# A transformer kernel of four blocks on one core: entry without the norm's factor, experts sent back in pairs, and GpSimd left with powers alone

## The chip, the cores and the metric

One of the eight cores of a Trainium2 chip runs the whole program. The metric is device time in microseconds (us) of one execution; 1 core means that there is no other core to wait for. TensorE multiplies, VectorE (DVE) and ScalarE (ACT) do elementwise work, GpSimd (POOL) too, and SyncE (SP) starts the transfers of weights.

## The reference

256 tokens of width 1024, batch 1, all in float32. Four blocks run one after another, each of which adds to x:

```python
h = rmsnorm(x, norm_mix[0]);  x += short_conv_mixer(h)     # layer 0
h = rmsnorm(x, norm_ffn[0]);  x += swiglu(h)               # 2816 wide
h = rmsnorm(x, norm_mix[1]);  x += mla_mixer(h)            # layer 1, 8 heads
h = rmsnorm(x, norm_ffn[1]);  x += moe_swiglu(h)           # 8 experts, 2 chosen, 2048 wide
h = rmsnorm_2(x, attn_norm_g); x += two_attentions(h)      # 8 query heads on 2 key heads; 4 differential heads
h = rmsnorm_2(x, mlp_norm_g);  x += square(relu(h @ w_up)) @ w_down    # 4096 wide

def rmsnorm(x, g):
    return x * rsqrt(mean(x * x) + EPS) * g
def short_conv_mixer(h):
    b, c, u = split(h @ w_in, 3)
    v = c * u
    conv = w[0] * v[t-2] + w[1] * v[t-1] + w[2] * v[t]
    return (b * conv) @ w_out
```

c, u and b are each linear in h, so a token's factor 1/rms can be left out of h: v then lacks the factor twice, 1/ms with ms = mean(x*x)+EPS, and the output lacks it once more. The expert block sends each token to the two best of eight experts, gathers an expert's tokens into up to 128 slots, and adds the gated results back.

## The kernel before

**Two halves of every number.** Float32 operands of the large products are split into a high part (w_hi, cast by ScalarE to fp32r, line 115) and the rest (w_lo, a subtraction on VectorE, line 116). A product is three: hi x hi, lo x hi, hi x lo (mm3, line 231). All weights pass through split() in the order that the generator weight_parts (line 159) writes out. load() (line 96) starts a transfer of 1 MB on SP's queue into one of RAW_BUFS = 7 raw buffers; during the expert stage three more (pool raws2, line 845) take turns with them, loads 8 to 10 of each ten (line 100). get() hands out the next split pair and keeps one more ahead; prepare(n) (line 216) makes sure that n are in the making. behind(...) and the list fence set an instruction behind others in the order that the framework's planner gives each engine; what is not so bound the planner orders by itself.

**Start.** x comes in four quarters of 128 tokens x 512 features, the first 128 tokens before the others (lines 65, 82). The gain row is spread over the partitions by a product with ones (line 560). first_norm (line 358) squares x on ScalarE, takes the power -1/2 on GpSimd (line 350), multiplies x by factor and gain on VectorE (line 374), transposes on TensorE (line 377) and splits into hT hi and lo (lines 379, 384). proj_T (line 236) makes 2 x 128 output features from two weight pairs, 24 products each. The conv loop (line 565) takes for each pair of feature blocks c (copied by ScalarE, line 568), u, then b, and forms the convolution on VectorE. Entry (line 397) is the transition to the next block: for each half of the tokens it adds the accumulated output to x (line 425), multiplies by the gain, transposes, splits, and takes squares and power; half(0) at once, half(1) in finish(), which the next block calls when its first products are issued.

**Experts** (line 1083). For g = 0 to 32, four chunks of 512 for each of 8 experts: gate and up of chunk g, then down of chunk g-1, which sums into two banks yb over an expert. When an expert's down is whole, gated_y (line 1049) splits yb into y; scatter (line 1057) sends it back to the tokens, 8 products of 512 columns and 4 additions into x, after gate and up of the next chunk. Every second expert, gather (line 1017) fetches the inputs of the next two by products with the 0/1 matrix pick, copied out by ScalarE (hi) and VectorE (lo). The last expert's scatter goes into the Entry of the second attention through enter (line 1126).

**Second attention** (line 1134). columns_in makes 256 columns of the input projection; the first call does one half of the tokens, then rest_of_entry, then the other. Generators keys_a, queries_a, heads_a and so on are advanced one step at a time by a table (line 1357), so that their steps alternate with the projections. rotate2 (line 1187) ends with an addition on GpSimd (line 1198); heads_a divides each head's exponentials by their sum on GpSimd (line 1301); the powers of all norms are GpSimd's too (lines 434, 1185, 1349). The differential heads divide on VectorE (line 1333).

Of the kernel before, what the change touches and what calls it, by code (L numbers as in the profile page):

```python
# [18 lines left out]
P = 128  # L19
# [22 lines left out]
def block_kernel(ctx: ExitStack, tc: tile.TileContext, i, out):  # L42
# [38 lines left out]
    for ns in blocks(2, 512):  # L81
        nc.sync.dma_start(x[:, 1, ns], i["x"][0, P:, ns])
# [43 lines left out]
    def columns_of(w):  # L126

        for c in range(0, w.shape[1], 256):
# [30 lines left out]
    def weight_parts():  # L159

        w = i["conv_w_in"][0]
        upper = [columns_of(w[:, g * D : (g + 1) * D]) for g in (1, 2, 0)]
        for _ in range(0, KD, 2):
            for u in upper:
                yield next(u)
                yield next(u)
# [69 lines left out]
    def proj_T(h, fresh=False):  # L236

        o = bank().rearrange("p (f t) -> p f t", f=2)
        for f in range(2):
            hi, lo = get()  # L240
            late, early = ((hi, h[1]), (lo, h[0])) if fresh and f == 0 else ((lo, h[0]), (hi, h[1]))
            for k in range(KD):
                mm(o[:, f], hi[:, k], h[0][:, k], k == 0, False)
            for k in range(KD):
                mm(o[:, f], early[0][:, k], early[1][:, k], False, False)
            for k in range(KD):
                mm(o[:, f], late[0][:, k], late[1][:, k], False, k == KD - 1)
        return o

# [108 lines left out]
    def first_norm(g):  # L358

        hi, lo = h_pair()  # L360
        xn = acts.tile([P, 2, D], F32, tag="xn", name="xn", bufs=1)
        factors = []
        for t in range(2):
            ss = small.tile([P, 2], F32, name="ss")
            for n, ns in enumerate(blocks(2, 512)):
                nc.scalar.activation(xn[:, t, ns], x[:, t, ns], AF.Square, accum_out=ss[:, n : n + 1])
            ms = small.tile([P, 1], F32, name="ms")
            nc.vector.tensor_scalar(ms, ss[:, 0:1], ss[:, 1:2], 1.0 / D, op0=OP.add, op1=OP.mult)
            nc.vector.tensor_scalar(ms, ms, EPS, None, op0=OP.add)
            factors.append(power(ms, 1))  # L370
        turned, copies = [], []
        for t, ts in enumerate(blocks(2)):
            for n, ns in enumerate(blocks(2, 512)):
                nc.vector.scalar_tensor_tensor(xn[:, t, ns], x[:, t, ns], factors[t], g[n], op0=OP.mult, op1=OP.mult)
                v = bank().rearrange("p (k t) -> p k t", k=4)
                for k in range(4):
                    nc.tensor.transpose(v[:, k], xn[:, t, (4 * n + k) * P : (4 * n + k + 1) * P], ident)
                hv, lv = (z[:, 4 * n : 4 * n + 4, ts] for z in (hi, lo))
                copies = copies[-1:] + [(nc.vector.tensor_copy if len(turned) == 3 else nc.scalar.copy)(hv, v)]
                turned.append((lv, v, hv))  # L380
        fence[:] = copies
        prepare(1)
        for lv, v, hv in turned:
            last = nc.vector.tensor_tensor(lv, v, hv.bitcast(F32), op=OP.subtract)
        fence[:] = [last]
        return hi, lo
# [10 lines left out]
    class Entry:  # L397
# [5 lines left out]
        def __init__(self):  # L403
# [3 lines left out]
            self.ss, self.ms, self.rs = (small.tile([P, 2], F32, name=n) for n in ("ss", "ms2", "rs2"))  # L407

# [10 lines left out]
        def enter(self, t, acc):  # L419
# [3 lines left out]
            for n, ns in enumerate(blocks(2, 512)):  # L423
                if acc is not None:
# [1033 lines left out]
```

## Time and profile before

| | |
|---|---|
| runs, us | 1303.44, 1300.73, 1299.24 (median 1300.73) |
| profiled execution | 1304.09 us, its span 1302.3 us, mean granted clock 0.992 |
| TensorE (PE) busy | 1267.9 us, 97% |
| VectorE busy | 994.9 us, 76% |
| ScalarE busy | 801.7 us, 62% |
| GpSimd busy | 76.3 us, 6%, 96 instructions |
| read from memory | 317 MB, 245 GB/s over the span |

A busy TensorE counts overlapping products once; where its share is whole, the pace of the products decides. "Idle before" a group is the time in which its engine did nothing just ahead of it, with the instruction that ended it. L377 is line 377 of the kernel.

### The profile page before, as it was taken

The numbers are of one execution on the slowest core, as the hardware profiler recorded it, in microseconds if no ns is written. First come the engines' busy times: TensorE is split into PE (matmuls) and PEld (weight loads), VectorE is DVE, ScalarE is ACT, GpSimd is POOL, SyncE is SP. The second block draws the span as 40 slices with busy tenths as digits, with TensorE's granted clock in tenths as the row PEclk, the third lists the DMA queues.
The fourth block names the chain that finished last, engine by engine and source line by source line (L and its number), as shares of the span: only waits on it lengthen the run. The fifth ranks groups of instructions, "written<-read, shape, count | busy, mean of one in ns | idle before, by whom it ended". The sixth has DMA issues, their size and how long they took to land.

```text
span 1302.3 us, 17506 instructions
## 1 busy us (share of the span) xinstructions
PE 1267.9 (97%) x6551; PEld 1065.9 (82%) x6551; DVE 994.9 (76%) x1283; ACT 801.7 (62%) x1089; POOL 76.3 (6%) x96
## 2 busy tenths in 40 slices
PE   8999999999998999999999999999998999999998
PEld 7998788888777888888888887878787887888887
DVE  6665655556867999999988989898898697765654
ACT  5444445445665877778867776777766566544442
POOL 0000100000502000000000000000000432000000
PEclk9999999999998999999999999999998999999999
DMA  9854655744434999989999999989987533456620
GB/s 318 280 168 175 217 192 129 245 142 149 163 127 174 372 379 353 374 306 360 356 335 320 326 359 337 349 324 361 349 307 243 177 106 114 144 188 196 192 97 33
DMA packets 156799, 320.26 MB, mean 246 GB/s; under 512 B 7788, under 2 KB 50823, under 8 KB 156712
## 3 DMA queue, kind: packets, MB, share of 16 engines
q1 hardware_dynamic: 151104, 313.54, 68.5%
q10 hardware_dynamic: 5608, 5.58, 1.8%
q8 instruction: 52, 0.85, 0.3%
q14 instruction: 35, 0.29, 0.1%
HBM read 317.00 MB, written 2.10 MB: 245 GB/s over the span
## 4 chain that ended last, share of the span: by engine, by line
PE 62%; DVE 2%; ACT 1%; POOL 1%; DMA 1%; issue 1%; POOLq 0%; ACTq 0%
PE bank L58 38%; PE yb L58 13%; PE acc L58 8%; PE bank L1076 1%; DVE w_lo L116 1%; PE po L58 1%; ACT w_hi L115 1%; DMA bias<-wide_d 1%; POOL yq L1198 0%; DMA raw<-in_moe_w_up_dram 0%; PE bank L1279 0%; POOL s L1301 0%; ACT s L1295 0%; POOL raq L1185 0%; PE bank L392 0%
## 5 line engine op out<-in xcount | busy, mean ns | idle before, releaser
L116 DVE TENSOR_TENSOR w_lo<-raw,w_hi 128x1024 fp32r<-128x1024 f32 (+2 forms) x600 | 709.6, 1218 | 189.6 <-ACT w_hi L115 177.4
L115 ACT CAST w_hi<-raw 128x1024 fp32r<-128x1024 f32 (+2 forms) x600 | 605.3, 1043 | 270.6 <-PE bank L58 149.1
L58 PE MATMUL bank<-w_hi,xT 128*128 128x512 f32 x1024 | 318.9, 393 | 0.9 <-ACT w_hi L115 0.9
L58 PEld LDWEIGHTS bank<-w_hi,xT 128*128 128x128 f32 x1024 | 190.4, 188 | 39.4 <-ACT w_hi L115 1.7
L58 PE MATMUL bank<-w_lo,xT 128*128 128x512 f32 x512 | 201.6, 394 | 1.1 <-DVE w_lo L116 1.1
L58 PE MATMUL bank<-w_hi,hT 128*128 128x256 f32 (+1 forms) x672 | 162.9, 338 | 2.4 <-ACT w_hi L115 2.0
L58 PEld LDWEIGHTS bank<-w_hi,hT 128*128 128x128 f32 x672 | 116.2, 192 | 15.8 <-ACT w_hi L115 2.3
L58 PE MATMUL bank<-hT,w_hi 128*128 128x256 f32 (+1 forms) x656 | 116.2, 326 | 2.2 <-DVE hT L394 1.4
L58 PEld LDWEIGHTS bank<-w_lo,xT 128*128 128x128 f32 x512 | 96.1, 188 | 26.2 <-DVE w_lo L116 6.4
L58 PE MATMUL bank<-w_lo,hT 128*128 128x256 f32 (+1 forms) x336 | 110.8, 337 | 0.0
L58 PEld LDWEIGHTS bank<-hT,w_hi 128*128 128x128 f32 x656 | 96.8, 194 | 11.1 <-DVE hT L394 1.7
L58 PE MATMUL yb<-w_hi,a_hi 128*128 128x512 f32 x256 | 101.3, 396 | 0.0
L58 PE MATMUL yb<-w_hi,a_lo 128*128 128x512 f32 x256 | 101.3, 396 | 0.0
L58 PE MATMUL yb<-w_lo,a_hi 128*128 128x512 f32 x256 | 95.6, 399 | 0.0
L58 PE MATMUL acc<-w_hi,a_hi 128*128 128x512 f32 x216 | 84.9, 393 | 0.0
L58 PE MATMUL acc<-w_lo,a_hi 128*128 128x512 f32 x216 | 84.4, 391 | 0.0
L58 PE MATMUL acc<-w_hi,a_lo 128*128 128x512 f32 x216 | 84.3, 390 | 0.0
L58 PEld LDWEIGHTS bank<-w_lo,hT 128*128 128x128 f32 x336 | 64.6, 192 | 6.9 <-DVE w_lo L116 0.5
L58 PE MATMUL bank<-hT,w_lo 128*128 128x256 f32 (+1 forms) x464 | 65.2, 284 | 0.0
L58 PEld LDWEIGHTS bank<-hT,w_lo 128*128 128x128 f32 x464 | 62.2, 194 | 2.3
L58 PEld LDWEIGHTS yb<-w_hi,a_lo 128*128 128x128 f32 x256 | 48.2, 188 | 11.3
L58 PEld LDWEIGHTS yb<-w_hi,a_hi 128*128 128x128 f32 x256 | 48.2, 188 | 11.4
(318 smaller groups left out, 1373.3 us busy)
## 6 DMA issues: line engine op xcount, KB each, us to landing
raw<-in_moe_w_gate_dram SPq DMA_DIRECT2D x64, 1024.0 KB, 6.5
raw<-in_moe_w_up_dram SPq DMA_DIRECT2D x64, 1024.0 KB, 6.6
raw<-in_moe_w_down_dram SPq DMA_DIRECT2D x64, 1024.0 KB, 6.4
raw<-in_w_up_dram SPq DMA_DIRECT2D x16, 1024.0 KB, 5.4
raw<-in_w_down_dram SPq DMA_DIRECT2D x16, 1024.0 KB, 4.9
raw<-in_conv_w_in_dram SPq DMA_DIRECT2D x12, 1024.0 KB, 12.1
raw<-in_ffn_w_gate_dram SPq DMA_DIRECT2D x11, 1024.0 KB, 5.1
raw<-in_ffn_w_up_dram SPq DMA_DIRECT2D x11, 1024.0 KB, 12.5
```

The costliest lines, as they stand in the source:

```text
L58: return nc.tensor.matmul(o, lhsT, rhs, start=start, stop=stop)
L115: halves[:] = [nc.scalar.copy(hv, v), nc.vector.tensor_tensor(lv, v, hv.bitcast(F32), op=OP.subtract)]
L116: nc.vector.tensor_tensor(lv, v, hv.bitcast(F32), op=OP.subtract)]
L1076: nc.tensor.transpose(bt[:, fs], sg[:, fs], ident)
```

## The change

The first weights of c_gate come as two loads of half a MB (512 rows x 256 columns each), and x comes by feature halves. first_entry transposes x itself, multiplies by the gain on the transposed side (a column per feature block), and splits. first_proj_T sums c's first two feature blocks by halves of the depth. 1/ms is put on a diagonal, spread to a row of 256 tokens by a product with ones, and multiplied into c; the root goes as a factor into the residual addition of the first Entry. In the expert stage two experts' rows are summed in one bank before they are added to x, in the last pair straight in the Entry; the first y of a pair lies in the tile "xn", the second takes a buffer of raws2; put has three buffers; gather copies on ScalarE alone. In the second attention the rotation's addition goes to VectorE, the division of the first head of a pair to ScalarE, of the second to VectorE.

```diff
-    for ns in blocks(2, 512):
-        nc.sync.dma_start(x[:, 0, ns], i["x"][0, :P, ns])
+    quarters = [(t, n) for n in range(2) for t in range(2)]
+    for t, n in quarters:
+        ns = blocks(2, 512)[n]
+        nc.sync.dma_start(x[:, t, ns], i["x"][0, t * P : (t + 1) * P, ns])
...
+        for rs in blocks(2, 512):
+            v = load(w[rs, D : D + 256], 4, 256)
+            for fs in blocks(2):
+                yield split(v[:, :, fs])
+        upper = [columns_of(w[:, g * D : (g + 1) * D], 256 * (g == 1)) for g in (1, 2, 0)]
...
+    def first_proj_T(h):
+        banks = [bank()[:, :T] for _ in range(2)]
+        for n in range(2):
+            for o in banks:
+                hi, lo = get()
+                for w, s in ((hi, 0), (hi, 1), (lo, 0)):
+                    for k in range(4):
+                        mm(o, w[:, k], h[s][:, 4 * n + k], n == 0 and k == 0 and w is hi and s == 0,
+                           n == 1 and k == 3 and w is lo)
+        return banks
...
-    def first_norm(g):
+    def first_entry(g):
...
+            for k in range(4):
+                turned = nc.tensor.transpose(v[:, k], x[:, t, (4 * n + k) * P : (4 * n + k + 1) * P], ident)
+            xgs.append(nc.vector.tensor_tensor(xg[:, j], v, g[:, 4 * n : 4 * n + 4, None].to_broadcast([P, 4, P]),
+                                               op=OP.mult))
...
+            his.append(nc.scalar.copy(place(hi, j), xg[:, j]))
...
+            los.append(nc.vector.tensor_tensor(place(lo, j), xg[:, j], place(hi, j).bitcast(F32), op=OP.subtract))
...
+        fence[:] = [his[2], los[1]]
+        prepare(2)
+        with behind(halves[0]):
+            rounded(3)
+        for j in (2, 3):
+            with behind(halves[1], los[-1]):
+                left(j)
+        fence[:] = [his[3], los[3]]
...
+    def first_factors(pool):
...
+                nc.scalar.activation(junk, x[:, t], AF.Square, accum_out=ss[:, t : t + 1])
+        nc.vector.tensor_scalar(ms, ss, 1.0 / D, EPS, op0=OP.mult, op1=OP.add)
+        nc.vector.reciprocal(inv, ms)
+        nc.gpsimd.tensor_tensor(rs, ms, mhalf[:, :2], op=OP.pow)
...
+            nc.vector.tensor_scalar(diag[:, t], ident, inv[:, t : t + 1], None, op0=OP.mult)
...
+                if acc is not None and self.factor is not None:
+                    nc.vector.scalar_tensor_tensor(x[:, t, ns], acc[n], self.factor[:, t : t + 1], x[:, t, ns],
+                                                   op0=OP.mult, op1=OP.add)
...
+                pc = first_proj_T(h)
+                first_rs, diag = first_factors(cp)
+                pu = proj_T(h)
+                b = bank()[:, :T]
+                with behind(products[-1]):
+                    mm(b, ones, diag.rearrange("p t k -> p (t k)"), True, True)
+                nc.scalar.copy(inv_row, b)
+                for f in range(2):
+                    nc.vector.tensor_tensor(c_sb[:, f], pc[f], inv_row, op=OP.mult)
+            else:
+                pc = proj_T(h)
+                nc.vector.tensor_tensor(c_sb, pc, inv_row[:, None, :].to_broadcast([P, 2, T]), op=OP.mult)
+                pu = proj_T(h)
...
-            for src, dst, copy in ((h_hi, x_hi, nc.scalar.copy), (h_lo, x_lo, nc.vector.tensor_copy)):
+            for src, dst in ((h_hi, x_hi), (h_lo, x_lo)):
...
-            put = ep.tile([P, T], F32R, name="put", bufs=2)
+            put = ep.tile([P, T], F32R, name="put", bufs=3)
...
+    def rows_back(rows, halves):
+            banks = [[bank() for _ in range(2)] for _ in halves]
+            for last, (put, y) in enumerate(rows):
+                for t, pair in zip(halves, banks):
+                    for s in range(2):
+                        for b, ns in zip(pair, blocks(2, 512)):
+                            mm(b, put[:, blocks(2)[t]], y[:, s, ns], last + s == 0, last + s == 2)
+            return banks
+        def scatter(rows):
+            for t in range(2):
+                for b, ns in zip(rows_back(rows, (t,))[0], blocks(2, 512)):
+                    nc.vector.tensor_tensor(x[:, t, ns], x[:, t, ns], b, op=OP.add)
...
-                if g == E * NC:
-                    prepare(3)
                 if c0 == NC - 1:
-                    done = gated_y(place, yb, g == E * NC)
+                    prepare(2)
+                    rows.append(gated_y(place, yb, len(rows) == 1))
...
+        for t, banks in enumerate(rows_back(rows, (0, 1))):
+            entry.half(t, banks)
+        prepare(4)
...
-            nc.gpsimd.tensor_tensor(dst, dst, tmp, op=OP.add)
+            nc.vector.tensor_tensor(dst, dst, tmp, op=OP.add)
...
-                nc.gpsimd.tensor_tensor(s, s, sm[:, :, None].to_broadcast([P, 2, T]), op=OP.mult)
+                for t in range(2):
+                    if c:
+                        nc.vector.tensor_scalar(s[:, t], s[:, t], sm[:, t : t + 1], None, op0=OP.mult)
+                    else:
+                        nc.scalar.activation(s[:, t], s[:, t], AF.Copy, scale=sm[:, t : t + 1])
```

## Rows read from the trace of the kernel before

**Rows 1.** Stretches: length, busy us (instructions) by engine, granted clock, DMA share, GB/s.

```profile
0.00:14.00 14.00, 7.50 (x22) 4.67 (x22) 5.78 (x17) 7.16 (x15) 2.67 (x11) 1.00 0.88 278
700.00:985.00 285.00, 283.00 (x1276) 228.62 (x1274) 254.79 (x253) 206.69 (x234) 0.00 (x0) 1.00 0.94 337
1003.00:1005.00 2.00, 2.00 (x11) 1.90 (x10) 2.00 (x4) 0.41 (x1) 0.00 (x0) 0.53 0.00 0
1026.00:1060.00 34.00, 31.82 (x257) 28.92 (x257) 29.34 (x60) 19.86 (x42) 15.60 (x9) 1.00 0.42 142
```

**Rows 2.** The start in order of time: start us, us, engine, line, operation.

```profile
7.61 0.63 ACT L366 ACTIVATE xn<-x 128x512 f32<-128x512 f32 x1 [0.71 <-DMA x<-in_x_dram]
8.72 0.75 DVE L374 SCALAR_TENSOR_TENSOR xn<-x,rs,bank 128x512 f32<-128x512 f32 x1
...
12.87 4.83 ACT L115 CAST w_hi<-raw 128x1024 fp32r<-128x1024 f32 x5
...
13.97 2.07 PE L58 MATMUL bank<-hT,w_hi 128*128 128x256 f32 x8 [0.77 <-ACT w_hi L115]
...
20.79 1.12 PE L58 MATMUL bank<-hT,w_lo 128*128 128x256 f32 x8
```

**Rows 3.** Transfers from 0 to 12 us: GB/s in 40 slices of 0.3 us.

```profile
GB/s 0 0 0 0 0 0 89 164 273 348 362 394 261 205 150 157 239 266 304 372 311 324 311 328 372 379 365 382 379 389 376 355 352 352 352 345 352 352 348 338
```

**Rows 4.** From the last expert to the second attention, in order of time.

```profile
994.50 1.26 ACT L228 ACTIVATE y<-yb,gslot 128x512 fp32r<-128x512 f32 x2 [2.35 <-PE yb L58]
995.22 1.41 DVE L229 SCALAR_TENSOR_TENSOR y<-yb,gslot,y 128x512 fp32r<-128x512 f32 x2 [0.56 <-ACT y L228]
...
997.88 1.28 DVE L1067 TENSOR_TENSOR x<-x,bank 128x512 f32<-128x512 f32 x2
...
999.90 1.94 PE L392 MATMUL bank<-ident,xg 128*128 128x128 f32 x8 [2.71 <-DVE xg L426]
...
1003.35 0.63 PE L58 MATMUL bank<-w_hi,hT 128*128 128x256 f32 x2
...
1007.70 0.99 PE L58 MATMUL bank<-w_hi,hT 128*128 128x256 f32 x3
```

**Rows 5.** Expert stage: a piece of the chain; SP's waits; weights' loads and differences.

```profile
439.62 5.60 PE yb L58 x24
...
SPq L104 <- DVE w_lo L116: 996.5, 273, 35.0
...
L116 DVE TENSOR_TENSOR w_lo<-raw,w_hi x378: 1214/1221/1228, 419.3 to 988.9; 128x1024 fp32r<-128x1024 f32 x189
...
DMA to landing us min/median/max: 5.1/6.6/8.5
```

**Rows 6.** TensorE's waits from 995 to 1125 us: total us, times, longest.

```profile
PE bank L1279 <- POOL s L1301: 2.2, 3, 1.3
PE bank L1205 <- POOL yq L1198: 1.5, 1, 1.5
...
PE bank L58 <- ACT s L1295: 1.3, 1, 1.3
```

**Rows 7.** Second attention: single lines (ns min/median/max, first and last start), pieces of time.

```profile
L1198 POOL TENSOR_TENSOR yq<-yq,tmp x2: 2172/3054/3937, 1021.4 to 1047.0; 128x512 f32<-128x512 f32 x2
L1301 POOL TENSOR_TENSOR s<-s,sm x8: 1040/1040/2028, 1039.4 to 1088.2; 128x512 f32<-128x512 f32 x8
L1333 DVE TENSOR_SCALAR s<-s,sm x8: 332/346/1208, 1058.2 to 1097.5; 128x256 f32<-128x256 f32 x8
L1334 DVE SCALAR_TENSOR_TENSOR s<-s,sm x8: 472/476/480, 1058.9 to 1098.2; 128x256 f32<-128x256 f32 x8
1046.86 5.41 DVE L116 TENSOR_TENSOR w_lo<-raw,w_hi 128x1024 fp32r<-128x1024 f32 x3
1058.20 1.64 POOL L1185 TENSOR_TENSOR rbq<-ss,mhalf 128x8 f32<-128x8 f32 x1 [5.03 <-DVE sm L1329]
1069.36 0.83 ACT L1263 ACTIVATE vb<-bank,rs 128x256 f32<-128x256 f32 x2
```

More of the change, by code (lines that the diff above doesn't have):

```diff
@@ L124, in rows_of, with columns_of @@
                 yield split(v[:, k : k + 1])
-    def columns_of(w):
-        for c in range(0, w.shape[1], 256):
+    def columns_of(w, begin=0):
+        for c in range(begin, w.shape[1], 256):
             v = load(w[:, c : c + 256], KD, 256)
@@ L240, in proj_T @@
             hi, lo = get()
[L241 to L247, printed above, removed]
-        return o
+            for w, s in ((hi, 0), (hi, 1), (lo, 0)):
+                for k in range(KD):
+                    products[:] = [mm(o[:, f], w[:, k], h[s][:, k], k == 0 and w is hi and s == 0,
+                                      k == KD - 1 and w is lo)]
+        return o
+    def first_proj_T(h):
[3 more added lines that the diff above has]
+                hi, lo = get()
+                for w, s in ((hi, 0), (hi, 1), (lo, 0)):
+                    for k in range(4):
+                        mm(o, w[:, k], h[s][:, 4 * n + k], n == 0 and k == 0 and w is hi and s == 0,
+                           n == 1 and k == 3 and w is lo)
+        return banks
     def proj(h, width, fresh=None, midway=None):
@@ new lines, in place, with rounded, left @@
+        def place(z, j):
+            t, n = quarters[j]
+            return z[:, 4 * n : 4 * n + 4, blocks(2)[t]]
+        def rounded(j):
+            his.append(nc.scalar.copy(place(hi, j), xg[:, j]))
+        def left(j):
+            los.append(nc.vector.tensor_tensor(place(lo, j), xg[:, j], place(hi, j).bitcast(F32), op=OP.subtract))
+        for j in range(4):
+            with behind(*los[-1:], *xgs[-1:]):
+                turned = multiplied(j)
+            if j < 3:
+                with behind(*his[-1:]):
+                    rounded(j)
+            if j == 1:
+                with behind(xgs[1]):
+                    left(0)
@@ L1047, in wide, with gated_y @@
             return b
-        def gated_y(place, yb, last):
-            y = room_y.tile([P, 2, D], F32R, tag="raw", name="y") if last else \
-                acts.tile([P, 2, D], F32R, tag="xn", name="y", bufs=1)
+        def gated_y(place, yb, odd):
+            y = (room_y if odd else acts).tile([P, 2, D], F32R, tag="raw" if odd else "xn", name="y",
+                                               **({} if odd else {"bufs": 1}))
             for n, ns in enumerate(blocks(2, 512)):
@@ L1081, in block_kernel @@
         gather(pick)
-        a = yb = place = done = None
+        a = yb = place = None
+        rows = []
         for g in range(E * NC + 1):
```

114 lines of the change are left out of this document (42 added, 72 removed).

## The prediction, made before the result was known

> **What bounds the kernel now.** I read the stretches by engine first. TensorE is busy 283.0 of 285 us in a stretch of the expert stage, where VectorE is busy 254.8 and ScalarE 206.7: what shortens VectorE's work there buys nearly nothing, since TensorE has 2 us to give [rows 1]. It idles where no product can start: in 0 to 14 us its 7.5 busy us are preparation, and in 1026 to 1060 us it is idle for 2.2 of 34 us while VectorE is busy 29.3 [rows 1]. So the change is worth what it takes from three gaps: the start, the step from the experts to the second attention, and the waits inside that attention. The rows of the start and of the end of the experts, in order of time, show the chains that fill the gaps; the list of TensorE's waits shows the third.
>
> **Part 1, the start.** Now the first product of a weight begins at 13.97 us. Before it lie the squares (the last quarter of x is read at 7.61), GpSimd's power, four multiplications by factor and gain on VectorE of 0.75 each, four groups of transposes, ScalarE's copies out of them, and only then, at 12.87, the first cast of a weight [rows 2]. The change takes x as it is: transpose, one multiplication by the gain, copy, difference; the factor 1/ms comes in later, and the factor's root at the residual. So the first product waits only for its weight.
>
> When does that arrive? The row of bytes moved has a value per 0.3 us; summed up, the 1.05 MB of x (and 16 KB of small rows) have been moved by 5.95 us, the first half MB behind them by 7.55, a whole MB by 9.0 [rows 3]. The last quarter of x was used at 7.61 [rows 2], 1.6 us after the last byte; so the new first load, half a MB, is there at 9.1. A cast of 512 columns costs what the squares do, 0.63 [rows 2]: first product at 9.8, 4.2 us earlier. The operand is ready: the first two quarters of x come before 7.61, and even the last one's four transposes (0.97), its multiplication (0.75) and the difference behind it (0.64, as the additions of that size [rows 4]) end at 10.0, when the third group of four products is still to come. Bounds: 4.9 us if the half MB is there at 8.4, when the order on ScalarE lets the cast start; 2.7 if it comes only with the whole (10.6). I take **-4.2**, nearest to the bytes' row.
>
> What is added: ScalarE's two squares of 1024 columns move behind the first weights, beside products; four multiplications by 1/ms replace ScalarE's copies on VectorE, 0.75 each, beside the 48 products of every projection; the product of ones with the diagonal is on TensorE's path. No row has its like; between 0.14 (a pitch of [rows 2]: 8 in 1.12) and 0.5 (twice what a 512-column product shows) I take **+0.25**. The first products run at about half rate now (8 in 2.07 us at 13.97, against 8 in 1.12 at 20.79 [rows 2]), though the granted clock reads 1.00 before 14 us [rows 1]; I leave that as it is. Should the earlier, thinner start stretch it, 28 more products at 0.1 would cost 2.8.
>
> **Part 2, the expert stage.** Sending rows back costs the same products: 16 for a pair of experts instead of twice 8. It saves 4 of 8 additions of 0.64 a pair [rows 4], and the gathers move 16 copies to ScalarE; both lie beside TensorE's work and I count them **0**. If VectorE's relief gave TensorE back its 2 idle us in 285, it would be -2 to -4 over the stage; if ScalarE's copies at the first gather delay the first expert by two copies of 0.63, +1.3. I take **+0.3**.
>
> The added wait is in the loads. The odd expert's y now takes one of the three extra weight buffers, from the end of its expert until its products are sent back: 24 products at 5.60 us [rows 5] make each of gate, up and down; so y is held for gate, up and the 16 products, some 15 us. SP's queue is in order, so the load that needs this buffer holds back all behind it. Counting the loads as the code issues them (ten buffers, 24 loads an expert), this is load 60, 110 and 158 of 192; the first is wanted by TensorE 25.5 us after its pair ends, the others 31. It is issued at 15, lands in 5.1 to 8.5 [rows 5], and needs 2.3 more for cast and difference: at 22.4 to 25.8, just in time the first time, 5 us early the others. SP has waits of up to 35 us for buffers already [rows 5], so loads are early now. **0**, with +0.3 as the bound from these rows.
>
> **Part 3, the last pair.** Today the last y is read out at 994.50, its second low part is ready 2.1 us later (995.22 and 1.41), x is added at 997.88 behind a weight's difference, multiplied, transposed at 999.90; the next products begin at 1003.35, the second token half's at 1007.70 [rows 4]. TensorE then still sits at half rate: 0.63 for a pair [rows 4], at a granted clock of 0.53, near the lower level of 1.2 GHz [rows 1]. After the change expert 6's eight products (1.8 us) no longer come before, so all is 1.8 earlier; they fill the wait for y, and both token halves' sums stand before the first addition. From the end of the last down product: low part 2.1; last two products of the first half 2.75; addition and gain, 0.6 each in a row, 4.0; four transposes 4.6; copy 5.3; low part 6.0; the other quarter 1.2 later, 7.2. Its 24 products run from 5.4 to 8.7. The second half then needs two additions and two multiplications on VectorE (8.4 for the first pair), transposes and a copy: products from 9.6 instead of 13.2, and their end is held to 13.1, against 16.4 now (13.2 and 24 products with their pauses). Gain 16.4-13.1+1.8 = 5.1. If the planner sets the two further weight differences (1.22 each) ahead of the second half, 2.7; if it mixes the halves well, 6. I take **-4.5**.
>
> **Part 4, the second attention.** TensorE waits 1.5 us for the rotated queries' addition on GpSimd and 2.2 for the division [rows 6]. These 11 instructions took 2.2 to 3.9 us for 512 elements of the sum, 1.04 to 2.03 for a division [rows 7]. The additions on VectorE cost 0.64 each like any of this shape [rows 4]; the divisions 0.35 (the same form in the other heads) on VectorE and about 0.42 on ScalarE, two each per pair [rows 7]. VectorE gets 3 x 0.6 + 8 x 0.35 = 4.6 us, ScalarE 8 x 0.42 = 3.4. VectorE also gets something back: three differences that ran beside GpSimd took 5.41 us where three of 1.22 [rows 5] are usual, and one division took 1.21 instead of 0.35 [rows 7]: 2.6 us in these rows alone. So its load hardly grows. Late next are the power (1.64, stays) and ScalarE's exponentials, whose wait of 1.3 us stays [rows 6]. Of the 3.7 us of waits I take **-3.5**; bounds -5 (the exponentials' 1.3 goes too) and +1 (three of the new 0.35 pieces in front of a weight's half that TensorE needs).
>
> One price depends on whether GpSimd's power, which stays, slows the new additions. The row shows no: eight sums of two products with two SBUF inputs take 472 to 480 ns, also the two that started inside a power (1058.20 to 1059.84) [rows 7]. The Trainium skill says otherwise ("SBUF — State Buffer", Who interferes with whom): a VectorE instruction with two SBUF inputs and a GpSimd one that reads SBUF exclude each other for the whole instruction. By that rule each addition behind a power would wait up to about 0.6 us, and part 4 would give some 1.8 less; this row does not agree, so the sum goes by the row.
>
> **Sum.** -4.2+0.25+0.3-4.5-3.5 = -11.65 us. The profiled execution took 1304.09, its span 1302.3 and 1.8 around it; it becomes 1292.4. The median shown is 1300.73, 3.4 lower; so 1289.0 us. A measurement of this kernel tells about 0.3% (3.9 us) from no change.
>
> **Rivals.** (a) *A gap only changes its owner.* In the attention, VectorE's 29.3 of 34 us [rows 1] leave little room, and a cast behind a division that waits for a sum is late: part 4 gives 0, 1292.5. Or the first half MB comes no earlier than the whole: part 1 gives -2.5, 1290.5; both 1294. For the second speaks that nothing shown has a half-size load. The Trainium skill ("DMA: Bandwidth & Descriptors", Queues, rings and completion order) says that completions of one queue are not in issue order over the 16 engines; no row here shows two small loads overtaking. Chance of some of this 0.18.
> (b) *Slower: starved experts.* If the planner sets y's products later than I place them by d, the first held load is 0.3+d us too late (its late landing), the two others d-5.2 each. Behind one more gate and up (d = 11) that is 11.3+5.8+5.8 = 23 us, less 11.7: 1312. It begins to cost at d = 0, has eaten the gain at 7.3 and shows as slower from 8.6 on. Against it: the planner put today's eight products where the code has them, and the loads are early. 0.06.
> (c) *No change.* The gaps close and the same time comes back as a longer half-rate start (2.8), a late gather (1.3 at each of four) and casts behind ScalarE's new work: 1297 to 1303. 0.06.
>
> **Numbers.** The forecast has 0.70, its own range 1284 to 1293. With (a), 1283 to 1296 holds 8 in 10. Faster by over 0.3% is the forecast and (a): 0.88; within 0.06; slower 0.06.
>
> **What would show it.** Right: first weight product at about 9.8 us; no idle of TensorE over 1 us behind GpSimd in the attention; the first products behind the experts some 5 us after the last down product; products of the expert stage as dense as now. Wrong: SP's wait of a raw load on y above 20 us followed by TensorE waiting for w_hi; w_hi casts late behind divisions; a first cast after 10.5 us.

## The result, and the profile after

| | before | after |
|---|---|---|
| median, us | 1300.59 (4 runs) | 1287.64 (4 runs, 1285.17 to 1290.47) |
| ratio, 95% interval | | 0.9899 [0.9876, 0.9921] |
| profiled execution; its span | 1304.09; 1302.3 | 1287.61; 1286.0 |
| TensorE, VectorE, ScalarE, GpSimd busy | 1267.9, 994.9, 801.7, 76.3 | 1257.8, 979.3, 812.7, 60.6 |

Predicted: 1289.0, range 1283 to 1296. The medians lie 12.95 us apart, the two spans 16.3. One event was taken at each boundary between stages, and the differences were set beside the prediction's terms:

| stretch, us | before | after | difference | predicted |
|---|---|---|---|---|
| start to first product with conv_w_out | 85.11 | 82.08 | -3.03 | -3.95 |
| to the first FFN's second transposes | 48.84 | 48.69 | -0.15 | 0 |
| to its first down product | 24.02 | 21.80 | **-2.22** | 0 |
| to the router | 242.62 | 242.61 | -0.01 | 0 |
| to the first gather | 9.96 | 8.74 | **-1.22** | 0 |
| to the end of the last down product | 584.15 | 580.20 | **-3.95** | -1.5 |
| to the squares of the keys | 18.02 | 16.20 | -1.82 | -2.7 |
| to the end of w_out_2's last product | 104.41 | 100.60 | -3.81 | -3.5 |
| to the end | 185.17 | 185.08 | -0.09 | 0 |

(-1.5 is +0.3 for the gather and the 1.8 of expert 6's products; -2.7 is the rest of -4.5.) Two of the three bold rows lie in code that the change doesn't touch. First the parts it does.

**The start**, rows of the changed kernel in order of time (start us, us, engine, line, operation, waits):

```profile
8.85 0.62 ACT L395 CAST hT<-xgT 128x512 fp32r<-128x512 f32 x1 [1.75 <-DVE xgT L386]
9.37 1.14 ACT L116 CAST w_hi<-raw 128x512 fp32r<-128x512 f32 x2
...
10.04 2.08 PE L58 MATMUL bank<-hT,w_hi 128*128 128x256 f32 x8 [0.86 <-ACT w_hi L116]
...
14.47 1.05 PE L58 MATMUL bank<-hT,w_lo 128*128 128x256 f32 x4
15.32 1.22 PE L58 MATMUL bank<-hT,w_hi 128*128 128x256 f32 x8
...
24.06 0.60 PE L58 MATMUL bank<-diag,ones_f 128*128 128x256 f32 x2
24.31 2.26 PE L58 MATMUL bank<-hT,w_hi 128*128 128x256 f32 x16
```

The first product begins 3.93 us earlier than at [rows 2]. Its cast follows ScalarE's copy of x without a pause, so the half MB was there. Then 25 products, up to 15.54, start some 0.21 us apart (the first pair 0.38), and the next ones 0.12. Before, 20 went so, from 13.97 to 18.40. The diagonal's products push the next by 0.25 (24.06 to 24.31).

**From the experts to the second attention**, the same view; the rows that answer to [rows 4]:

```profile
983.96 2.95 PE L58 MATMUL bank<-y,put 128*128 128x512 f32 x12
984.65 1.41 DVE L235 SCALAR_TENSOR_TENSOR y<-yb,gslot,y 128x512 fp32r<-128x512 f32 x2 [1.50 <-ACT y L234]
986.25 1.28 DVE L479 TENSOR_TENSOR x<-x,bank 128x512 f32<-128x512 f32 x2 [0.19 <-PE bank L58]
...
988.19 1.32 PE L441 MATMUL bank<-ident,xg 128*128 128x128 f32 x8 [1.28 <-DVE xg L480]
989.52 0.39 PE L58 MATMUL bank<-w_hi,hT 128*128 128x256 f32 x1
...
991.38 2.35 DVE L117 TENSOR_TENSOR w_lo<-raw,w_hi 128x1024 fp32r<-128x1024 f32 x2
993.65 0.68 DVE L479 TENSOR_TENSOR x<-x,bank 128x512 f32<-128x512 f32 x1
994.38 0.38 PE L58 MATMUL bank<-w_hi,hT 128*128 128x256 f32 x1 [0.68 <-ACT hT L442]
```

The last down product ends at 984.12; the next block's first product starts 5.40 us later, where it was 8.65. But two further weight differences, 2.35 us, run ahead of the second half's last addition (993.65), and that half's first product comes only 10.26 us after the last down product.

**TensorE's waits** from 975 to 1125 us in the changed kernel (total us, times, longest), beside [rows 6]; and the stretch of the second attention, in the changed kernel and then in the one before:

```profile
PE bank L58 <- DVE hT L443: 2.1, 3, 1.4
PE bank L58 <- DVE s L1386: 1.7, 1, 1.7
PE bank L1266 <- issue: 1.5, 1, 1.5
PE bank L441 <- DVE xg L480: 1.3, 1, 1.3
```

```profile
1000.32:1100.92 100.60, 96.53 (x688) 83.57 (x687) 82.81 (x190) 66.60 (x155) 17.37 (x12) 1.00 0.37 125
1012.72:1117.13 104.41, 98.06 (x690) 84.00 (x689) 83.06 (x179) 63.44 (x147) 32.67 (x23) 1.00 0.35 117
```

No wait names GpSimd any more; its busy time there is 17.37 us (32.67 before). In their place TensorE waits 1.5 us, instead of 0.5, for the keys' transposes (VectorE makes their operand, now behind its own rotation addition and a weight's difference), and the score products of the differential heads wait 1.7 us behind VectorE's sums with the bias (L1386), where they waited 1.3 behind the exponentials (L1295 in [rows 6]). In this stretch TensorE's idle time fell from 6.35 us (104.41 less 98.06) to 4.07.

**The expert stage** is denser, against the second of [rows 1]:

```profile
690.00:975.00 285.00, 284.12 (x1292) 231.85 (x1292) 251.65 (x242) 215.27 (x245) 0.00 (x0) 1.00 0.92 343
```

**The stretch at 130 us**, which the change doesn't touch: the same product and 20 us around it, in the kernel before and then in the changed one.

```profile
137.02 1.40 PE L58 MATMUL bank<-w_hi,hT 128*128 128x512 f32 x4 [2.03 <-ACT w_hi L115]
...
130.00:150.00 20.00, 17.97 (x76) 14.29 (x75) 12.30 (x12) 10.35 (x13) 5.61 (x10) 0.91 0.67 202
```

```profile
133.03 1.19 PE L58 MATMUL bank<-w_hi,hT 128*128 128x512 f32 x4 [1.22 <-ACT w_hi L116]
...
128.00:148.00 20.00, 18.71 (x85) 15.04 (x85) 12.55 (x12) 12.09 (x14) 5.64 (x10) 1.00 0.75 236
```

TensorE waited for a weight in both; where it waited 2.0 us, a stretch at half rate followed. Whether that is luck or the change's doing, the experiments had to say.

### The profile page after: what moved, and what is told of

Same layout as the page of the kernel before. It is cut to its first block, busy times and chain, and to the rows that moved or that the text cites. A ratio compares the mean times of both kernels' runs of the same rounds, so it can differ in the third digit from the quotient of the medians.

```text
span 1286.0 us, 17514 instructions
## 1 busy us (share of the span) xinstructions
PE 1257.8 (98%) x6550; PEld 1061.2 (83%) x6550; DVE 979.3 (76%) x1269; ACT 812.7 (63%) x1109; POOL 60.6 (5%) x84
## 4 chain that ended last, share of the span: by engine, by line
PE 61%; DVE 4%; ACT 1%; issue 1%; DMA 0%; POOL 0%; POOLq 0%; ACTq 0%; DVEq 0%
PE bank L58 39%; PE yb L58 13%; PE acc L58 8%; DVE w_lo L117 1%; PE bank L1140 1%; DMA raw<-in_moe_w_up_dram 0%; DVE s L1386 0%; DVE mx L1388 0%; DVE mx L1352 0%; ACT s L1356 0%; PE po L58 0%; DVE hT L443 0%; POOL rs L1246 0%; DVE ss L1238 0%; ACT s L1390 0%
## 6 DMA issues: line engine op xcount, KB each, us to landing
raw<-in_conv_w_in_dram SPq DMA_DIRECT2D x11, 1024.0 KB, 12.9
```

## The experiments

Each kernel ran beside the kernel before on the same chip. "The attention" below is the time from the keys' squares to the end of w_out_2's last product (104.41 before, 100.60 after).

### One part at a time

```diff
# start_only: the kernel before, with
+            v = load(w[rs, D : D + 256], 4, 256)
...
-        h = first_norm(g)
+        h, turned = first_entry(cols[:, 32 : 32 + KD])
```

> The kernel before with the first part of the change alone (x transposed as it is, half-size first loads, factor 1/ms later). Theory (three gaps, each closed by its own part): first product of a weight at 10.0 us instead of 13.97, first conv_w_out product 3.0 earlier (82.1 instead of 85.11), span shorter by 3 to 4 us and no more: the second attention as long as before (keys' squares to last product of w_out: 104.0 us). Rival (the wait for a weight at 135 us is tied to the start): the wait of 2.0 us for w_hi at the end of the first FFN chunk and the half-rate products behind it shrink here too, the first router product comes 5.4 earlier (395.2 instead of 400.59), and the span is 5 to 6.5 us shorter. If that wait differs from execution to execution, it comes out between the two.

Measured: median 1297.46 against 1300.09 (12 and 24 runs), ratio 0.998 [0.9966, 0.9993], so -2.6 us. First product at 9.56, first conv_w_out product at 81.59, 3.5 earlier. The wait at 130 us was 1.52, with a granted clock of 0.83 from 130 to 140, and that stretch took 23.68 us. The profiled run was the slowest of the twelve (1303.08; a clock under 0.97 in five ten-us slices behind 990 us), so its later stretches say little: the attention took 105.68.

```diff
# experts_only: the kernel before, with
+                    nc.scalar.copy(dst[:, k0 : k0 + 2], v)
...
+                    rows.append(gated_y(place, yb, len(rows) == 1))
...
+        for t, banks in enumerate(rows_back(rows, (0, 1))):
+            entry.half(t, banks)
```

> The kernel before with the second and third part alone (rows sent back by pairs, gather's copies on ScalarE, the last pair's sums before the first addition). Theory: nothing moves up to the router; the first expert's first product is 0.3 to 0.5 later against the first gather; from there to the first product of the second attention 583.6 us instead of 586.83 less some tenths (3 to 3.8 us gained, 1.8 of them expert 6's eight products); what follows is no longer than before; span 2 to 4 us shorter, ratio 0.997 to 0.9985. Rival (starved by the held buffer): TensorE waits for w_hi behind a raw load held by y, the expert stage is longer by 5 us or more. Rival (gap changes owner): gain at the first product but keys' squares less than 1 us earlier.

Measured: median 1295.37, ratio 0.9963 [0.9949, 0.9976], -4.7 us: more than expected. From the first expert's product to the second attention's first 579.42 us, 7.4 less than before instead of 3 to 3.8. The transition gives its part (5.39 us from the last down product to the first product; keys' squares at 16.19); the rest came in the experts' own stretch, 580.43 from the gather to the last down product against 584.15. The attention took 104.42, as before. No wait for a weight is over 0.5 us: nothing is starved.

```diff
# attn_only: the kernel before, with
-            nc.gpsimd.tensor_tensor(dst, dst, tmp, op=OP.add)
+            nc.vector.tensor_tensor(dst, dst, tmp, op=OP.add)
...
+                        nc.vector.tensor_scalar(s[:, t], s[:, t], sm[:, t : t + 1], None, op0=OP.mult)
...
+                        nc.scalar.activation(s[:, t], s[:, t], AF.Copy, scale=sm[:, t : t + 1])
```

> The kernel before with the fourth part alone (rotation's additions on VectorE, division on ScalarE and VectorE). Theory: TensorE's waits behind GpSimd's sums and divisions (3.7 us) go; keys' squares to last product of w_out 100.2 to 100.8 us instead of 104.0, span 3 to 4 us shorter. Rival (gap changes owner: VectorE full): 103 to 104 us, span within 1 us of before.

Measured: the attention 100.62 us, as the theory had it; median 1294.80, ratio 0.9953 [0.9935, 0.9971]. Here too the start is the old one, and yet the stretch at 130 us took 21.78 (wait 1.20), and it took 21.86 in the kernel with the experts' part alone. **So its 2.2 us are no effect of the change**: of the 14 profiles, three had it long (before 24.02, start_only 23.68, busy_start 23.98; two of them with the changed start), with the longest waits for that weight (2.0, 1.5 and 2.4 us against 1.20 to 1.35). The same goes for the way from the router to the first gather (9.96 before, 8.74 in the changed kernel): with the code of before it took 8.82 in this kernel, 8.73 in experts_only and 9.40 in start_only. The three ratios' distances from 1 add to 1.04%, the whole change's is 1.01%: the parts add, within their intervals. One thing of the attention shows already here, beside the old transition: TensorE waits 1.3 us at the keys' transposes.

### The start

How far two profiles of the same start lie apart has to be known first. Nine profiles have the changed start without an edit in it: the first product comes at 9.47 to 10.13 us, 14 to 25 products go at half rate, and the first conv_w_out product comes at 81.01 to 82.08 (median 81.34; the changed kernel's own profile is the latest of them). Three have the start of before: 13.55 to 14.20, 20, 19 and 1 products at half rate, 83.72 to 85.11 (median 84.66).

```diff
# whole_first_load: the changed kernel, with
-        for rs in blocks(2, 512):
-            v = load(w[rs, D : D + 256], 4, 256)
+        v = load(w[:, D : D + 256], KD, 256)
+        for rs in blocks(2, 4):
             for fs in blocks(2):
-                yield split(v[:, :, fs])
+                yield split(v[:, rs, fs])
```

> The changed kernel with its first weight loaded as one whole MB instead of two halves; all else at the start as changed. Theory (the first product waits for its bytes): first product at 11.2 to 11.8 us instead of 10.0, since the whole MB is moved 1.45 us after the half one. Rival (the order on ScalarE, copies of x ahead of the first cast, decides): 10.0 to 10.4.

```profile
10.60 1.14 ACT L116 CAST w_hi<-raw 128x512 fp32r<-128x512 f32 x2 [1.74 <-DMA raw<-in_conv_w_in_dram]
...
11.27 2.07 PE L58 MATMUL bank<-hT,w_hi 128*128 128x256 f32 x8 [2.31 <-ACT w_hi L116]
```

The cast, free since 8.86, waits for the load and begins at 10.60; the first product at 11.27. Beside the nine profiles the half load is worth 1.1 to 1.8 us at the first product and 1.1 to 2.2 at the first conv_w_out product (83.21), by one profile.

```diff
# busy_start: the changed kernel, with
+            for _ in range((4, 4, 5, 3)[j]):
+                mm(v[:, 0], ones, ones, True, True)
             for k in range(4):
                 turned = nc.tensor.transpose(v[:, k], ...
...
+        for _ in range(5):
+            mm(banks[0][:, :P], ones, ones, True, True)
```

> The changed kernel with 21 products of ones by ones, 128 columns each, between the transposes of x and ahead of the first weight's product, in TensorE's waits; nothing reads them. In the changed kernel the products from 10.04 to about 15.3 us go at half rate, 24 of them at 0.21 us instead of 0.12, 2.2 us lost. Theory (the rate is half because TensorE stood idle before): with TensorE busy from 2.5 us on the first weight's products go at full rate, first conv_w_out product at 80 us instead of 82.08, first product not later than 10.5; span 1 to 2 us shorter. Rival (the chip starts at half rate whatever TensorE does): the same 24 products at half rate, and 0.2 to 0.8 us later through the filling.

```profile
11.09 1.19 PE L58 MATMUL bank<-hT,w_hi 128*128 128x256 f32 x8
...
132.78 2.08 PE L58 MATMUL bank<-w_hi,hT 128*128 128x512 f32 x4 [2.38 <-ACT w_hi L116]
```

This agrees with the theory's cause: with TensorE busy from 2.6 us on, the first weight's eight products take 1.19 us instead of 2.08. But attn_only, with the start of before and nothing filled in, had its first eight at the full rate, too:

```profile
14.20 1.22 PE L58 MATMUL bank<-hT,w_hi 128*128 128x256 f32 x8 [1.07 <-ACT w_hi L115]
```

So one profile doesn't show that it was the filling. The filling delays the products to 11.09, and the first conv_w_out product comes at 80.70, 0.3 to 1.4 earlier than in the nine. Nothing of this arrives: median 1292.30, ratio 0.9938 [0.9919, 0.9957], some 5 us above the changed kernel. The profiled run (1290.39) shows two places: at 130 us TensorE waits 2.38 us for a weight and goes on at half rate (23.98 us, one of the three above), and the attention took 101.47. What the slower runs lost, no profile shows.

### The experts

```diff
# own_y: the changed kernel, with
-            y = (room_y if odd else acts).tile([P, 2, D], F32R, tag="raw" if odd else "xn", name="y", ...
+            y = (parts if odd else acts).tile([P, 2, D], F32R, tag="y_odd" if odd else "xn", name="y", bufs=1)
```

> The changed kernel with the odd expert's y in a buffer of its own instead of one of the three extra weight buffers. Theory (holding it costs nothing, its cover is the loads that are far enough ahead): the gaps in SP's loads of up to 17 us behind a pair shrink, but from the first expert's first product to the last down product it stays 573.7 us, within 0.5. Rival (b) in small: TensorE's few waits for weights go, 0.5 to 1.5 us shorter.

SP's waits from 412 to 985 us, in this kernel and then in the changed one:

```profile
SPq L105 <- DVE w_lo L117: 481.4, 185, 8.1
```

```profile
SPq L105 <- DVE w_lo L117: 422.8, 161, 18.0
SPq L105 <- PE bank L58: 31.0, 3, 13.8
SPq L105 <- DVE y L235: 10.6, 4, 4.7
```

SP's longest wait falls from 18.0 to 8.1 us, and the waits for y and for the rows' products go; gather to last down product takes 579.91 us against 580.20. From the first expert's product on it is 573.49, against 573.66 to 574.28 in the eight profiles with this stage as changed: holding the buffer costs 0.8 us at most.

```diff
# send_back_later: the changed kernel (put with four buffers), with
-            if len(rows) == 2:
+            if len(rows) == 2 and c == 0:
                 scatter(rows)
```

> The changed kernel with the pair's rows sent back one gate, up and block of down products later (24 products at 5.60 us three times: 16.8 us later), so the odd expert's y holds a weight buffer for 32 us instead of 15. Rival (b) of the prediction, with its price: first held load 17.1 us too late, the two others 11.6 each, expert stage longer by about 40 us, with TensorE waiting for w_hi behind loads that SP issued late. If the loads are further ahead than the prediction counted them: some 10 us later than counted gives about 10 us in all, enough slack gives less than 1.

```profile
720.00:740.00 20.00, 17.53 (x77) 13.71 (x77) 15.43 (x16) 11.14 (x14) 0.00 (x0) 0.97 0.42 152
740.00:780.00 40.00, 38.29 (x168) 30.98 (x167) 32.23 (x32) 27.68 (x31) 0.00 (x0) 0.97 0.89 335
```

The edit did more than its expectation says: an expert has four chunks, so the condition next holds three chunks on. The products that send rows back start at 624.97, 771.36 and 919.91 instead of 573.51, 718.34 and 865.12, so y is held some 50 us longer, not 16.8. One run: 1294.13, and 586.76 us from gather to last down product, 6.6 more than the changed kernel. There are waits for w_hi of 1.7 and 1.6 us, most of the loss behind the second pair (720 to 780: 4.2 us idle at a clock of 0.97). By the price of rival (b) it would have been over 100 us. The mechanism is there, the place was wrong: the load that needs y's buffer goes out right behind y's products (624.97 and 3.89), but SP has issued 18 loads since 577 us before it, so it pauses some 6 us, not for the whole time of holding:

```profile
614.14 8.38 SPq L105 DMA_DIRECT2D raw<-in_moe_w_up_dram  x2
628.90 0.94 SPq L105 DMA_DIRECT2D raw<-in_moe_w_down_dram  x2
```

Of the experts' 192 loads it is the 81st; in the changed kernel the one that goes out right behind y's products (573.51 and 3.89, issued at 577.43) is the 63rd, near the prediction's 60. So the price of rival (b) failed in its load number: it let the same load wait however long y is held, and here a later one waits.

```diff
# gather_shared: the changed kernel, with
-            for src, dst in ((h_hi, x_hi), (h_lo, x_lo)):
+            for src, dst, copy in ((h_hi, x_hi, nc.scalar.copy), (h_lo, x_lo, nc.vector.tensor_copy)):
...
-                    nc.scalar.copy(dst[:, k0 : k0 + 2], v)
+                    copy(dst[:, k0 : k0 + 2], v)
```

> The changed kernel with the gather's copies shared by ScalarE and VectorE again, as before. Theory of the prediction: the first gather to the first expert's product 0.3 to 0.6 us shorter (6.51 in the changed kernel, 5.97 before), the rest of the expert stage as long as now (573.7), since VectorE's relief buys nothing. Rival (the relief of VectorE is where the expert stage gained more than expert 6's 1.8 us): the stage is 0.8 to 2 us longer.

Gather to last down product: 581.18, 0.98 longer, though the first gather itself is a little shorter (its second half's products and the first expert's 2.41 us apart instead of 2.96, of which 0.4 is only that four small products come before it in the changed kernel). From the first expert's product on it is 575.22, against 573.66 to 574.28 in the eight profiles with this stage as changed. So moving the 16 copies off VectorE is worth about 1 us (0.9 to 1.6, by one profile): the rival's side. (Its 1289.81 also holds a half-rate stretch at 990 us, keys' squares at 17.72.)

### The second attention

```diff
# add_on_gpsimd: the changed kernel, with
-            nc.vector.tensor_tensor(dst, dst, tmp, op=OP.add)
+            nc.gpsimd.tensor_tensor(dst, dst, tmp, op=OP.add)
```

> The changed kernel with the rotation's three additions back on GpSimd, divisions left where the change put them. Theory (each wait behind GpSimd is paid by itself): TensorE waits some 1.5 us for the rotated queries again; from the start of the keys' squares to the end of the last w_out product 101.7 to 102.6 us, against 100.60 in the changed kernel and 104.41 before. Rival (division alone made the gap, additions are hidden): under 100.9. Second rival (the chain is shared, one slow step gives it all back): 103.5 or more.

```diff
# division_on_gpsimd: the changed kernel, with
-            for c, (s, sm) in enumerate(probs):
+            for s, sm in probs:
                 nc.vector.reciprocal(sm, sm)
...
+                nc.gpsimd.tensor_tensor(s, s, sm[:, :, None].to_broadcast([P, 2, T]), op=OP.mult)
```

> The changed kernel with the division by the sums back on GpSimd, additions left on VectorE. Theory: TensorE waits 2.2 us for divided scores again; keys' squares to last w_out product 102.4 to 103.2 us, against 100.60. Rival (the additions alone made the gap): under 100.9. Together with the run beside it the two differences should add up to the 3.8 us by which the change shortened the stage.

TensorE's waits behind 980 us with the additions on GpSimd, then with the divisions:

```profile
PE bank L58 <- DVE s L1386: 2.6, 1, 2.6
...
PE bank L1266 <- POOL yq L1259: 1.6, 1, 1.6
...
PE po L58 <- ACT vb L1324: 1.1, 1, 1.1
```

```profile
PE po L58 <- ACT vb L1324: 2.1, 1, 2.1
...
PE bank L58 <- ACT s L1356: 0.8, 1, 0.8
```

Medians 1290.29 and 1292.76; the attention 103.13 and 104.24: +2.53 and +3.64, over what was expected, and 6.2 together where 3.8 were to be shared. Both profiles show a slower clock between 1050 and 1080 us. Three kernels with the changed attention had such a stretch too (own_y, whole_first_load, busy_start), and it took 101.44 to 101.47 in them, 0.86 more than the 100.60 to 100.62 of the four without (the changed kernel, attn_only, gather_shared, send_back_later). Less that, 1.7 and 2.8 are left, near the theory's 1.5 and 2.2, and 4.4 in all. So each part seems to pay for itself, the division the more; that the slower clock is luck in these two as well is taken over from the other three, not shown. The division's wait comes back in another place than it left: not at the transposes (0.2 us named GpSimd) but at the products behind ScalarE's vb. At the keys' transposes TensorE waits 0.8 us with the additions on GpSimd and 1.5 with the divisions there: 0.7 of that wait came with the additions on VectorE.

### A version beyond the change

```diff
# second_half_first: the changed kernel, with
-        prepare(4)
+        entry.between = lambda: prepare(2)      # called in entry.half(1) behind its last multiplication
...
-            ws = (get(), get())
+            ws = (get(), get()) if bias else (ready.pop(0), ready.pop(0))
```

> The changed kernel, but the two further weight differences (w_lo) of the second attention are taken behind the second token half's multiplications instead of ahead of them. Theory (VectorE's order bounds the second half): the second half's last low part is ready about 2.4 us earlier, TensorE's waits for hT behind the first products go (2.1 us in all in the changed kernel), keys' squares come 1 to 2 us earlier than 10.8 us behind the first product; span 1 to 2 us below the changed kernel's 1286.0, ratio to the kernel before 0.988 to 0.9895. Rival (the weights then come late): TensorE waits for w_lo or w_hi at the second block of columns instead, no gain: within 0.5 us of 1286.0.

```profile
PE bank L1270 <- issue: 2.2, 1, 2.2
PE bank L58 <- DVE hT L443: 1.7, 2, 1.4
...
1000.00:1010.00 10.00, 7.80 (x53) 7.62 (x53) 9.28 (x23) 4.27 (x6) 2.66 (x2) 0.83 0.51 157
```

The second half's products follow the first's without a pause, and the keys' squares come at 15.12 us instead of 16.20. The gap only moved on: the wait at the keys' transposes grew from 1.5 to 2.2, the clock fell to 0.83 behind it, and the attention took 102.27. Median 1288.47, ratio 0.9902 [0.9883, 0.992]: nothing gained.

```diff
# second_half_first_later_turn: that kernel, and in keys_a
             yield
+            yield
             turn(akT, yd.rearrange("p t j c d -> p t j (c d)"), nc.scalar.copy)
```

> The kernel in which the second half's multiplications come before the further weight differences, and the keys' transposes moved behind the second block of queries' products as well. In the run without the latter TensorE stood 2.2 us before the keys' transposes and had a granted clock of 0.83 in the 10 us around it. Theory (a gap that changed its owner): both go, keys' squares to last w_out product 99 to 100 us instead of 102.27, span 1282.5 to 1284, 2 to 3.5 us below the changed kernel's. Rival (the first scores then wait for the keys): a wait of 1 us or more in front of the scores, no gain against 1286.

```profile
999.68:1098.05 98.37, 95.85 (x684) 83.08 (x683) 81.73 (x189) 65.51 (x154) 21.65 (x12) 1.00 0.38 125
...
PE bank L58 <- DVE s L1391: 1.7, 1, 1.7
```

With the keys' transposes one block later no wait is left there, no new one came before the scores, and the attention takes 98.37 us, span 1283.1. But the keys' squares, where it begins, come 16.63 us behind the last down product, against 16.20 in the changed kernel and 15.12 in the version above, with a slower clock on the way:

```profile
990.00:1000.00 10.00, 10.00 (x74) 10.00 (x74) 6.76 (x11) 3.60 (x7) 0.54 (x1) 0.85 0.64 205
```

From the last down product to the end of w_out_2 it is 115.00 us against the changed kernel's 116.80. Median 1285.13 (1284.76 to 1285.55), ratio 0.9889 [0.9869, 0.9908]. The span is 2.9 us shorter than the changed kernel's, 1.8 of it here and 1.1 ahead of the first conv_w_out product (81.01 against 82.08), in code that this edit leaves alone; the ratios lie 0.1% apart and their intervals overlap, so as a time it is not told apart from it.

## Why the prediction was right

**The sum held, its terms less.** Without the two stretches that are chance (-2.22 and -1.22) the stages add to -12.9 us; the forecast was -11.65, the medians give -12.95. Those 3.44 us are about what the profiled execution of before stood above its median (3.36), so setting the sum against its own time and then going over to the median was right, too. That the total came so near is in part luck: parts 1 and 3 gave 2.7 us less than taken, part 2 gave 3.3 more.

**Part 1, taken -4.2 + 0.25, was -3.03.** First product (10.04, predicted 9.8), half load, diagonal (0.25) and the bound of the whole load (cast at 10.60, predicted 10.6) are right. In this pair the step that gave way is the one left "as it is", the half rate at the start: 25 products instead of 20 go so, 0.5 us, between the 0 taken and the 2.8 named. But this number changes from profile to profile of the same start (14 to 25), so it isn't shown that the earlier start stretched it. By the medians of the nine and three profiles (81.34 and 84.66) the part gave 3.3 us.

**Part 2, taken +0.3, was about -3.** The 0 for the products was the failed step, and its own bound, -2 to -4 if VectorE's relief gave TensorE back its idle time, is what happened. From the gather to the last down product, before and after:

```profile
410.55:994.70 584.15, 582.15 (x2664) 476.45 (x2664) 532.35 (x527) 440.21 (x489) 3.47 (x2) 1.00 0.94 340
403.92:984.12 580.20, 579.33 (x2661) 476.62 (x2662) 515.00 (x495) 449.54 (x505) 3.48 (x2) 1.00 0.92 343
```

VectorE's busy time fell from 532.35 to 515.00 us, TensorE's waits for w_hi and w_lo from 2.0 to 0.8, and the same products took some 2 us less. About one us is the gathers' copies; that the rest is the additions saved wasn't tried. The first gather cost about 0.1, not 0.3. Of expert 6's eight products four came back as early ones of the last pair: 0.9 us gained here, not 1.8. The held buffer was rightly counted about 0 (0.8 us at most by own_y); rival (b), built on it, was priced far too high.

**Part 3, taken -4.5, was about -2.7: the bound that the prediction gave for the planner's setting two weight differences ahead of the second half**, and just this is what it did. The failed step is the place of these two differences. First products came 5.40 us after the last down product, predicted 5.4; the second half's at 10.26, predicted 9.6. Moved away (second_half_first), the keys' squares came 1.1 us earlier, and the keys' transposes waited 0.7 longer. The clock has a share, too: all three profiles of the old transition show a slower stretch in it (granted clock 0.73 to 0.90 from 990 to 1000 us). Of the nine of the changed one, seven have the keys' squares 16.19 to 16.21 us behind the last down product; gather_shared and division_on_gpsimd, with a clock of 0.83 and 0.84 there, have them at 17.72 and 17.70, hardly earlier than the 18.02 of before.

**Part 4, taken -3.5, was -3.81**, alone and in the whole. The 3.7 us of waits behind GpSimd are gone, as predicted. Rival (a) is there in small: 1.0 us more at the keys' transposes and 0.4 more at the score products. That the sum came out even so has a term that the prediction didn't have: of 3.81 us, 2.28 were idle time and 1.5 busy time, and 1.0 of this is the 32 products of va with the divided scores. They took 6.04 us before and in experts_only, 5.03 in the changed kernel and in attn_only, 6.07 with the divisions back on GpSimd.

**The power beside VectorE's additions.** The prediction took them at full speed, by one row. In the changed kernel (GpSimd and VectorE in order of time):

```profile
1007.01 1.65 POOL L1246 TENSOR_TENSOR raq<-ss,mhalf 128x8 f32<-128x8 f32 x1 [4.14 <-DVE ss L1244]
...
1007.97 1.22 DVE L117 TENSOR_TENSOR w_lo<-raw,w_hi 128x1024 fp32r<-128x1024 f32 x1
1009.10 0.69 DVE L1259 TENSOR_TENSOR yq<-yq,tmp 128x512 f32<-128x512 f32 x1
...
1042.38 1.21 DVE L117 TENSOR_TENSOR w_lo<-raw,w_hi 128x1024 fp32r<-128x1024 f32 x1
1042.42 2.67 POOL L1246 TENSOR_TENSOR rbq<-ss,mhalf 128x8 f32<-128x8 f32 x1 [10.91 <-DVE sm L1394]
```

A weight's difference that starts inside a power takes 1.22 us, the usual [rows 5]; a power that starts 0.04 us behind a difference takes 2.67 instead of 1.64, and the next power behind one (1051.46) does, too. So a power doesn't hold VectorE up; GpSimd's power is held up, by about one difference. Beside GpSimd's additions and divisions of 512 elements it was otherwise: three differences took 5.41 us there [rows 7]. The Trainium skill ("SBUF — State Buffer", Who interferes with whom) lets either exclude the other for a whole instruction; beside the powers this trace agrees in the one direction alone, and the 1.8 us by that rule didn't come.

## What to carry to other kernels

Read what one gap is worth from the chain that closes it, and ask at once what the planner will set into the freed time: the second half's delay came from weight differences that were free to move up, and part of the keys' wait from an addition that the change itself had put on VectorE. An engine that is busy nine tenths beside a bound one is no cover that costs nothing: taking 17 of VectorE's 532 us away went with 3 us fewer for TensorE. Compare stages between two traces before comparing spans: here 3.4 of 16.3 us were one execution's bad luck in code that nobody touched. And take the scatter of a stage from every profile that has it unchanged: the same start differed by 1.1 us, as much as some effects looked for in it.

## What the runs showed of the hardware beyond that

The stretches at half rate that were looked at stand behind waits of TensorE, and they go with the scatter between runs: of start_only's, one with a span of 1294.4 us had a mean granted clock of 0.996, the one with 1301.3 had 0.990. The product that waited 1.20 to 1.35 us at 130 us went on at a clock of 1.00 in that slice; those that waited 1.5 to 2.4 us had 0.83 to 0.89. But the length of a wait doesn't decide by itself: in the transition to the second attention the changed kernel and division_on_gpsimd have the same listed waits (1.3, 0.3, 0.7 and 0.3 us), with a clock of 1.00 in the one and 0.84 in the other. The four runs of the last version lie within 0.8 us of each other, the 24 of before within 8.3. At the start the granted clock reads 1.00 from 0 to 14 us, in the kernel before and after, while the products go at half rate, so it tells nothing there; the pitch of the products does. How many go at half rate differs between executions of the same start (14 to 25), and once, in attn_only, the first eight were at the full rate without a product more ahead of them. And a gain at the start needn't show in the span: busy_start's profile was up to 1.4 us ahead at 80 us, and a longer wait for a weight at 130 us with the half rate behind it cost it 2.2.
